# A batch-normalised matmul on one core: the order of its 782 tasks read from a table, and one small negation on GpSimd

## The chip, the core and the metric

The kernel runs on one core of a Trainium2 chip. The metric is device time in microseconds (us); the median of 3 runs of the kernel before is 206.29 us (206.23 to 206.86). Engines are written as in the profile: PE (TensorE matmul), PEld (its weight loads), DVE (VectorE), ACT (ScalarE), POOL (GpSimd), SP (SyncE, which here only issues DMAs).

## The reference

```python
def setup_inputs():
    batch, m, k, n = 16, 512, 1024, 768
    return {"x": randn(batch, m, k), "weight": randn(k, n), "gamma": ones(n), "beta": zeros(n), "eps": 1e-5}

def reference(x, weight, gamma, beta, eps):
    y = np.matmul(x, weight)
    mean = np.mean(y, axis=(0, 1), keepdims=True)
    var = np.var(y, axis=(0, 1), keepdims=True)
    return gamma * (y - mean) / np.sqrt(var + eps) + beta
```

All in float32. There are 8192 rows of y and 768 columns, and a column's mean and variance need all 8192 rows. So no element of a column can be written before the last matmul of that column is done.

## The kernel before

**Tiling.** The rows are 16 chunks (c = 0 to 15) of 512. The columns are six blocks of 128 (nt = 0 to 5, "column 0" to "column 5" below). Columns 0 and 1 are computed first, with rows on the partitions (`mm_rows`, L501 to L517), while x is still being loaded; columns 2 to 5 of chunks 0 to 3 are computed in this stage too. From about 97 us on the loads are over. Then come the last matmuls of columns 0 and 1 (`ga_unit`, L805, chunks 14 and 15), the sums and the scale and shift of these two columns (L865 to L915), and after that the rest of column 2, then 3, 4 and 5 (`col_unit`, L627, matmuls at L575, four weight tiles of 256 rows of k each, in two halves of four matmuls).

**One unit.** A unit (one chunk of one column) fills one of the 8 PSUM banks. Its statistics are taken (DVE bn_stats, L711; in column 2 from chunk 4 on two ACT passes with sums, L720 and L724), it is copied to SBUF as bf16 (ACT, L715), and then its bank is free. After a column's last unit, `finish_tasks` makes scale and shift (L976, L990, L993 to L998; for column 2 on ACT, L1004 to L1007, with the negated gamma of L964).

**Out again.** A finished column is normalised in SBUF (L1024 on ACT for column 2, L1026 on DVE for 3 and 4, L1348 for 5) and must be transposed back to rows: by a transposing DMA from the SP queue (L1220) and a copy to float32 on ACT (L1232); or on PE (`turn_block`, L1044, into a PSUM bank) and a copy on ACT (L1210, L1252, L1361). Some blocks are transposed raw beforehand (L1106) and normalised afterwards by DVE (L1174) and GpSimd (L1178). Columns 0 and 1 leave by DVE (L937), an add on GpSimd or DVE (L942) and a store (L946). All stores are issued by SP, in order, 512 KB each for the most part; the loads of x and of the weights by GpSimd. Two blocks of column 4 (chunks 14 and 15) are held back on purpose until the end (`held_block`, L1240).

**Riders.** The eight PE transposes of a column-4 block need not be a task of their own: a column-5 half may carry up to four of them, one after each of its matmuls (`mm`, L571 to L584). In the kernel before four blocks ride, four and four in consecutive halves.

**Who sets the order.** The code makes 786 tasks, each with a due time, possible engines with costs, dependencies, and the slots (PSUM banks, SBUF tiles, ring space) that it takes and uses. `arrange` (L122) is a greedy planner: it models the engines, the DMA queue (`Wires`) and a port that DVE tasks marked `lock` and GpSimd share (L162 to L165), and picks, at the earliest time at which some engine can begin something, the ready task with the smallest due time. The emitted instructions of each engine are then chained in this order by `seq` (L293), so each engine, and SP's queue of DMAs, runs its list in order; an instruction whose input is late holds up all that stand behind it on its engine.

**Names the change touches.** `negate_gamma` (L963, the task `ng`), whose result is read at L1004; `terms` (L1317), three small GpSimd instructions of column 5, first used at L1324; the copies of `part_chunk` (L547) that lay out chunks 12 to 15 plainly for columns 4 and 5 and may run on DVE or ACT.

Of the kernel before, what the change touches and what calls it, by code (L numbers as in the profile page):

```python
# [97 lines left out]
class Wires:  # L98
# [8 lines left out]
    def ready(self, queue):  # L107
        lanes = self.lanes[queue]
        return 0.0 if len(lanes) < self.LANES else lanes[-self.LANES]
# [9 lines left out]
        return t, land  # L119


def arrange(tasks, turns, log=None):  # L122

    free = {e: 1.25 for e in ("PE", "DVE", "ACT", "POOL", "SP")}
    wires = Wires()
    port = {"DVE": 0.0, "POOL": 0.0}
    left = sorted(tasks, key=lambda t: t.prio)
    order = []  # L130
    SEM, LOOK = 0.06, 0.2

    def ready(t):
        if t.after is not None and t.after.end is None:
            return None
        r = 0.0
        for d in t.deps:
            if d.end is None:
                return None
            r = max(r, d.end + SEM + t.slack)  # L140
        kept = [(s.pool, s.pool.mark()) for s in t.takes] if len(t.takes) > 1 else []
        fits = True
        for s in t.takes:
            p = s.pool.place(s)
            if p is None:
                fits = False
                break
            r = max(r, p[0] + SEM)
            if kept:
                s.pool.take(s, p[1])  # L150
        for pool, mark in reversed(kept):
            pool.reset(mark)
        if not fits:
            return None
        if t.dma:
            r = max(r, wires.ready(list(t.engines)[0]))
        return r

    def start_of(t, r, e):

        b = max(r, free[e])
        if e == "DVE" and t.lock:  # L162
            b = max(b, port["POOL"])
        elif e == "POOL" and not t.dma:
            b = max(b, port["DVE"])  # L165
        return b

    while left:
        seen = [(t, ready(t)) for t in left]
        first = {}  # L170
        for t, r in seen:
            if r is not None:
                for e in t.engines:
                    b = start_of(t, r, e)
                    if e not in first or b < first[e]:
                        first[e] = b
        if not first:
            raise RuntimeError(f"nothing can begin: {[(t.prio, t.emit) for t in left[:8]]}")
        e = min(first, key=lambda k: first[k])
        best = None  # L180
        for t, r in seen:
            if r is not None and e in t.engines and start_of(t, r, e) <= first[e] + max(LOOK, t.look):
                if best is None or t.prio < best[1]:
                    best = start_of(t, r, e), t.prio, t
        start, _, t = best
        for s in t.takes:
            s.pool.take(s, s.pool.place(s)[1])
        occ, lat = t.engines[e]
        t.hosted = []
        if t.hosts:  # L190
            room = t.hosts
            for u, r in seen:
                if u in turns and r is not None and r <= start + 0.3 and room >= 1:
                    n = min(room, turns[u][0])
                    if turns[u][0] == turns[u][1]:
                        places = [s.pool.place(s) for s in u.takes]
                        if any(p is None or p[0] > start for p in places):
                            continue
                        for s in u.takes:
                            s.pool.take(s, s.pool.place(s)[1])  # L200
                        u.takes_done, u.takes = u.takes, []
                    t.hosted.append((u, n))
                    turns[u][0] -= n
                    room -= n
                    occ += 0.0555 * n
                    lat += 0.0555 * n
        if t in turns:
            occ = lat = 0.0555 * turns[t][0]
            lat += 0.2
            t.count = turns[t][0]  # L210
        free[e] = start + occ
        if e == "DVE" and t.lock or e == "POOL" and not t.dma:
            port[e] = start + occ
        t.end = start + lat
        if t.dma:
            free[e], t.end = wires.send(e, start, occ, t.dma, t.count)
        t.start, t.engine = start, e
        order.append(t)
        left.remove(t)
        for u, n in t.hosted:  # L220
            if turns[u][0] == 0:
                u.end = t.end + 0.2
                left.remove(u)
    return order


# [1 line left out]
def kernel(  # L228
# [9 lines left out]
    nc = tc.nc  # L238
# [3 lines left out]
    ALU = mybir.AluOpType  # L242
# [5 lines left out]
    P = 128  # L248
# [44 lines left out]
    def seq(bi):  # L293

        ins = bi.ins
        prev = last.get(ins.engine)
        if prev is not None:
            tc.add_manual_dep(
                ins, prev,
                mybir.DependencyInfo(mybir.DependencyClass.NoSync, mybir.DependencyReason.DATA),  # L300
                reason="order",
            )
        last[ins.engine] = ins.name
        return bi

    gamma_sb = singles.tile([P, NT], f32)
# [28 lines left out]
    ngamma = singles.tile([P, NT], f32)  # L335
# [17 lines left out]
    tasks, turns = [], {}  # L353
    banks, xts, ys, sqs, rings = Pool(8), Pool(XT), Pool(YB), Pool(SQ), Space(RING)

    def task(prio, engines, emit, deps=(), lock=False, **kw):
        t = Task(prio, engines, emit, deps, **kw)
        t.lock = lock
        tasks.append(t)
        return t  # L360

    def dve(occ):
        return {"DVE": (occ, occ + 0.09)}
# [4 lines left out]
    def pool(occ):  # L368
        return {"POOL": (occ, occ + 0.05)}
# [70 lines left out]
    order = [("x", 0), ("w", 0, 2), ("x", 1), ("w", 2, 4)]  # L440
# [5 lines left out]
    t = 1.0  # L446
    affine = None
# [237 lines left out]
    def y_of(nt, c):  # L685
        return y_col.setdefault((nt, c // GY), Slot(ys))
# [174 lines left out]
    S = clock[0]  # L861
# [61 lines left out]
    sr = task(U + 0.1, dve(0.35), shift_rows, [sc], True)  # L923
# [32 lines left out]
    k = 0  # L956
# [4 lines left out]


    def negate_gamma(eng):  # L963
        seq(nc.vector.tensor_scalar(ngamma, gamma_sb, -1.0, None, op0=ALU.mult))  # L964

    ng = task(S, dve(0.1), negate_gamma, [affine, sr], True)

    def finish_tasks(nt):
        deps = [col_end[nt, c][0] for c in range(C)]
# [61 lines left out]
    def turn_block(prio, nt, m0, count, deps, uses):  # L1031

        bank = Slot(banks)
        todo = []

        def step():
            if not todo:
                o_ps = psum.tile([P, count, P], bf16, tag="b")
                bank.tile = o_ps
                for s in range(count):  # L1040
                    c, i = divmod(m0 // P + s, RT)
                    todo.append((o_ps[:, s], y(nt, c)[:, i * P:(i + 1) * P]))
            dst, src = todo.pop(0)
            seq(nc.tensor.transpose(dst, src, ident))  # L1044

        def emit(eng):
            for _ in range(emit.task.count):
                step()

        emit.step = step  # L1050
        t = task(prio, pe(0.0555 * count), emit, deps, takes=[bank], uses=uses)
        emit.task = t
        turns[t] = [count, count]
        return t, bank
# [213 lines left out]
    for nt in range(GA, NT - 1):  # L1268
# [10 lines left out]
        f = finish_tasks(nt)  # L1279
        start = clock[0] + 3.0  # L1280
# [58 lines left out]
    for c, r0, rows in ends:  # L1339
        due = E + 2.0 + 0.6 * c  # L1340
        n = max(rows // CH, 1)
# [13 lines left out]
        b, bank = turn_block(due + 0.6 * (n - 1), nt, m0, count, norms, [y_of(nt, c + i) for i in range(n)])  # L1355
# [7 lines left out]
        def store(eng, slot=slot, m0=m0, count=count):  # L1363
# [6 lines left out]
             uses=[slot])  # L1370

    order = arrange(tasks, turns)
    if "PLAN" in globals():
        PLAN.append(order)
# [37 lines left out]
```

## Time and profile before

The profiled execution has a span of 204.1 us from its first to its last instruction; the median of the three timed runs is 206.29 us, so 2.2 us lie around the span.

| engine | busy us | share of the span | instructions |
|---|---|---|---|
| PE | 189.3 | 93% | 1210 |
| DVE | 159.3 | 78% | 250 |
| ACT | 146.2 | 72% | 260 |
| POOL | 124.1 | 61% | 150 |
| DMA | 303 GB/s to and from HBM over the span | 36.7 MB read, 25.2 MB written | |

A row of the table of groups gives a line, an engine, an operation, how often, its busy time and the mean duration of one. A row of the timeline gives start, length, engine, line and operation; overlapping instructions of one line are merged. "Busy" for PE is modelled from the starts, so a stall of a few tens of nanoseconds doesn't show in it; the distance between starts does.

### The profile page before, as it was taken

How to read it: one execution, taken by the hardware profiler on the slowest of the kernel's cores; microseconds unless marked ns; L12 is line 12 of the kernel's file. 1: busy time of each engine (PE TensorE's matmuls, PEld its weight loads, DVE VectorE, ACT ScalarE, POOL GpSimd, SP SyncE). 2: the span in 40 equal slices, each digit the busy share in tenths (PEclk: the TensorE clock that was granted, in tenths of full speed). 3: DMA queues.
4: the chain of work that ended last, by engine and by line, in shares of the span. 5: the costliest groups of instructions: out<-in, count | busy, mean ns of one | idle time of the engine just before them, and what ended most of it. 6: DMA issues, size and time to landing. Idle time of an engine off the chain costs nothing.

```text
span 204.1 us, 3510 instructions
## 1 busy us (share of the span) xinstructions
PE 189.3 (93%) x1210; PEld 114.5 (56%) x1210; DVE 159.3 (78%) x250; ACT 146.2 (72%) x260; POOL 124.1 (61%) x150
## 2 busy tenths in 40 slices
PE   7969999999999999999999999999999999997900
PEld 3457554657488888777865444444444445544600
DVE  4031879999999999969989998987999878657900
ACT  2001461368989999899978766999998959956950
POOL 7776954877499989997403999389613312940000
PEclk9999999999999999999999999999999999999965
DMA  4999999999999999999686899899999999999998
GB/s 71 172 199 196 176 196 196 196 197 197 190 193 197 197 196 196 196 197 195 103 181 200 297 339 336 248 301 328 295 322 227 336 303 274 347 343 310 310 347 253
DMA packets 98562, 48.74 MB, mean 239 GB/s; under 512 B 24304, under 2 KB 98032, under 8 KB 98544
## 3 DMA queue, kind: packets, MB, share of 16 engines
q0 software_dynamic: 34624, 18.36, 65.5%
q1 hardware_dynamic: 63920, 30.16, 52.6%
q8 instruction: 9, 0.15, 0.3%
q14 instruction: 9, 0.07, 0.1%
HBM read 36.71 MB, written 25.17 MB: 303 GB/s over the span
## 4 chain that ended last, share of the span: by engine, by line
PE 86%; ACT 3%; DMA 3%; POOL 2%; issue 1%; ACTq 0%; DVE 0%; POOLq 0%
PE y_ps L575 54%; PE y_ps L510 24%; PE y_ps L814 4%; ACT o_sb L1361 3%; DMA ring<-in_x_dram 3%; PE o_ps L1044 1%; POOL ring L403 1%; POOL w_sb L387 1%; PE y_ps L753 1%; PE a_ps L903 1%; PE o_ps L1074 0%; ACTq L1407 0%; PE idle_ps L591 0%; PE tot_ps L871 0%; ACT ring L1252 0%
## 5 line engine op out<-in xcount | busy, mean ns | idle before, releaser
L575 PEld LDWEIGHTS <-w_sb 128*128 128x128 bf16 x520 | 50.3, 97 | 57.6
L575 PE MATMUL y_ps<-xT_sb,w_sb 128*128 128x512 bf16 (+1 forms) x272 | 59.3, 371 | 0.0
L575 PE MATMUL y_ps<-x_pl,w_sb 128*128 128x512 bf16 x248 | 57.4, 379 | 0.0
L403 POOL DMA_DIRECT2D ring<-in_x_dram x76 | 47.2, 626 | 14.4 <-DMA ring<-in_x_dram 5.5
L510 PE MATMUL y_ps<-w_sb,xT_sb 128*128 128x256 bf16 x448 | 50.6, 273 | 1.7 <-DMA ring<-in_x_dram 1.6
L510 PEld LDWEIGHTS <-xT_sb 128*128 128x128 bf16 x448 | 43.5, 98 | 9.4 <-DVE xT_sb L435 2.9
L435 DVE STREAM_TRANSPOSE xT_sb<-ring 128x1024 f32<-128x1024 f32 (+1 forms) x29 | 31.2, 1111 | 14.1 <-DMA ring<-in_x_dram 13.9
L711 DVE BATCH_NORM_STATS2 stats<-y_ps 128x6 f32<-128x512 f32 x46 | 30.9, 687 | 7.7 <-PE y_ps L575 7.2
L715 ACT CAST y_sb<-y_ps 128x512 bf16<-128x512 f32 x51 | 29.0, 593 | 10.4 <-DVE stats L711 6.3
L547 ACT COPY x_pl<-xT_sb 128x1024 bf16<-128x1024 bf16 x32 | 32.8, 1063 | 1.7 <-DVE xT_sb L435 1.7
L942 POOL TENSOR_TENSOR ring<-ring,sum 128x1024 f32<-128x1024 f32 (+1 forms) x11 | 23.8, 2188 | 14.9 <-ACT y_ps L724 10.9
L659 ACT ACTIVATE sq_sb<-y_ps 128x512 f32<-128x512 f32 x28 | 16.3, 610 | 16.2 <-PE y_ps L510 15.9
L666 POOL TENSOR_TENSOR sum<-sum,sq_sb 128x512 f32<-128x512 f32 x20 | 25.6, 1278 | 3.0 <-ACT sq_sb L659 1.7
L662 DVE TENSOR_TENSOR sum<-y_ps,sum 128x512 f32<-128x512 f32 x28 | 18.9, 675 | 6.3 <-ACT sq_sb L659 5.3
L672 ACT CAST y_sb<-y_ps 128x512 bf16<-128x512 f32 x28 | 16.3, 594 | 8.2 <-DVE sum L662 8.0
L1178 POOL TENSOR_TENSOR ring<-ring,sum 128x1024 f32<-128x1024 f32 x6 | 14.8, 2477 | 9.8 <-issue 8.5
L937 DVE TENSOR_TENSOR ring<-y_sb,a_ps 128x1024 f32<-128x1024 bf16 (+1 forms) x16 | 16.7, 1079 | 0.1
L1044 PE MATMUL o_ps<-ident,y_sb 128*128 128x128 bf16 x104 | 13.1, 221 | 1.6 <-DVE y_sb L1348 1.5
L1232 ACT CAST ring<-ring 128x1024 f32<-128x1024 bf16 x13 | 13.8, 1063 | 0.6 <-DMA ring<-y_sb 0.6
L1145 POOL COPY sum<-sum 32x256 f32<-32x256 f32 (+1 forms) x17 | 5.8, 340 | 13.4 <-DVE sum L1142 6.5
L428 DVE STREAM_TRANSPOSE xT_sb<-ring 128x2048 bf16<-128x2048 bf16 x6 | 13.5, 2290 | 0.1
L591 PE MATMUL idle_ps<-idle_sb 128*128 128x512 f32 x18 | 9.6, 688 | 1.5 <-DVE idle_sb L316 1.5
(104 smaller groups left out, 153.7 us busy)
## 6 DMA issues: line engine op xcount, KB each, us to landing
out_dram<-ring SPq DMA_DIRECT2D x37, 512.0 KB, 3.4
ring<-in_x_dram POOLq DMA_DIRECT2D x52, 256.0 KB, 8.8
out_dram<-o_sb SPq DMA_DIRECT2D x6, 512.0 KB, 4.7
ring<-in_x_dram POOLq DMA_DIRECT2D x16, 128.0 KB, 5.9
w_sb<-in_weight_dram POOLq DMA_DIRECT2D x8, 192.0 KB, 6.2
out_dram<-ring SPq DMA_DIRECT2D x6, 256.0 KB, 3.0
ring<-in_x_dram POOLq DMA_DIRECT2D x4, 192.0 KB, 7.8
out_dram<-o_sb SPq DMA_DIRECT2D x3, 256.0 KB, 2.5
```

The costliest lines, as they stand in the source:

```text
L403: bi = seq(nc.gpsimd.dma_start(x_bf[32 * i:32 * i + 32], src[:, :, KQ * i:KQ * (i + 1)]))
L435: seq(nc.vector.transpose(dst, src[:, :, jw0:jw1]))
L510: seq(nc.tensor.matmul(y_ps[:, s], x_of(c, jw, e, t * P, (t + 1) * P), w_sb[:, jw, e, 0:NA], start=(s == 0 and jw == 0 and e == 0), stop=( ...
L547: seq(nc.scalar.copy(dst, pairs) if eng == "ACT" else ENG[eng].tensor_copy(dst, pairs))
L575: seq(nc.tensor.matmul(y_ps, w_sb[:, jw, e, nt * P:(nt + 1) * P], moving(c, jw, e, q0 * QR, q1 * QR, parted), start=(jw == 0 and e == 0 an ...
L659: seq(nc.scalar.activation(sq_sb[:, 0:n], slot.tile[:, 0:n], AF.Square))
L662: seq(nc.vector.tensor_add(sum1, slot.tile[:, 0:n], sum1))
L666: seq(ENG[eng].tensor_add(acc, acc, state["sq"][:, 0:n]))
L711: seq(nc.vector.bn_stats(dst, slot.tile))
L715: seq(nc.scalar.copy(y(nt, c), slot.tile))
L937: seq(nc.vector.tensor_mul(slot.o, y_row[c].y[:, s0:s1], aff[0][:, None, :].to_broadcast([P, n, NA])))
L942: seq(ENG[eng].tensor_add(slot.o, slot.o, row[:, None, :].to_broadcast([P, n, NA])))
```

## The change

The greedy choice in `arrange` goes. In its place a table `ORDER` names every task by its number (in order of creation) after a letter for its engine (P PE, V DVE, A ACT, G POOL, S SP); what follows a plus sign are riders, "658.3" for three transposes of task 658. The costs, slots and dependencies stay: slots are still assigned by the same rule as the list is walked. The table came from a search in which transfers were made longer at random. And the negation of gamma is a GpSimd instruction.

```diff
+ORDER = (
+    "G0 P59 G3 G8 A9 G4 G7 V1 V2 P60 G10 P61 P62 P63 P64 P65 V5 V6 P66 G12 P67 P68 P69 P70 P71 G14 P76 A72 "
...
+    "A274 G54 A276 P403 P404 A281 V49 P405 A250 P406 P409 G278 V50 A261 P285 A262 V283 G57 V277 P290 A286 "
+    "V282 A279 V288 A284 V287 P410 A291 P411 V52 A289 G293 P412 A263 P415 G320 G321 G322 G381 P295 P298 V292 "
+    "V53 V319 V299 V296 A401 A413 A414 A264 A297 A402 A294 A300 A407 P304 P301 P323 V55 V58 V56 P310 P307 "
...
+    "V339 V336 V342 G340 G337 P420 P423 P389 P443 P435 P424 P444 P436 A390 A421 A422 A417 A445 A418 A437 A425 A446 "
+    "V345 V343 V351 V348 S341 S391 S344 S338 G346 G349 S347 P427 P439 P431 P440 P428 P432 P447 P448 A441 A426 "
+    "A429 A442 A433 A449 A434 V352 V354 S353 S350 G355 V360 V357 G358 S356 V361 V369 V363 A430 A438 A450 S362 "
...
+    "G542 V587 V606 V610 V602 V586 V585 V588 V589 V614 V591 G543 A550 A544 A603 A590 A611 A615 P620 P621 P632 "
+    "P633 P628 P629 P636 P637 S561 S557 S555 S551 V545 G546 A558 S547 V626 V618 V622 V634 V568 V564 V630 V638 "
+    "V641 S565 S559 A627 A631 A607 A642 A562 A635 A639 A619 A623 P673 P681 P682 P674 S569 V643 V661 V657 V644 "
+    "V665 V683 A566 A645 S563 P685+658.3 P689+662.1 P686+658.2,662.1 P677+662.1,658.1 P701+658.2,662.1 P678 "
+    "P690+662.4 S573 G646 A684 A570 A647 A659 S567 S571 V687 V651 V669 V648 V675 V679 V691 V654 S660 A574 "
+    "A663 A676 A688 A692 A680 S575 G652 G649 G655 P697 P698 P705 P706+670.3 P702+670.2,666.1 P709+670.1,666.2 "
+    "P693+666.1,670.2 P694+666.4 P713 P710 V707 V729 V695 V703 V699 V711 A671 A667 A708 A696 S664 S650 S656 "
+    "S653 S668 S672 P714 P717 P720 V723 V715 V718 V721 P730 P733 V724 V726 A712 A700 A704 A716 A731 A725 V728 "
...
+)
...
-    left = sorted(tasks, key=lambda t: t.prio)
+    left = tasks
     order = []
-    SEM, LOOK = 0.06, 0.2
+    SEM = 0.06
...
-    while left:
-        seen = [(t, ready(t)) for t in left]
...
-        start, _, t = best
+    NAMES = {"P": "PE", "V": "DVE", "A": "ACT", "G": "POOL", "S": "SP"}
+    for word in ORDER.split():
+        word, _, riders = word.partition("+")
+        t, e = left[int(word[1:])], NAMES[word[0]]
+        r = ready(t)
+        if r is None:
+            raise RuntimeError(f"out of order: {word}")
+        start = start_of(t, r, e)
...
-        if t.hosts:
...
+        for rider in riders.split(",") if riders else ():
+            i, n = rider.split(".")
+            u, n = left[int(i)], int(n)
...
     def negate_gamma(eng):
-        seq(nc.vector.tensor_scalar(ngamma, gamma_sb, -1.0, None, op0=ALU.mult))
-
-    ng = task(S, dve(0.1), negate_gamma, [affine, sr], True)
+        seq(nc.gpsimd.tensor_scalar(ngamma, gamma_sb, -1.0, None, op0=ALU.mult))
+
+    ng = task(S, pool(0.3), negate_gamma, [affine])
```

Set beside the order of the kernel before, engine by engine, the table reads as follows. Up to about 97 us every engine has the same list. From there on:

- PE: the same 196 tasks. The last two units of columns 0 and 1 and the sums change places (P304 P301 P323). The units of column 2 from chunk 9 on, of column 3, 4 and 5 are taken out of the order of their chunks, with halves of several units interleaved: P443 P435 P424 P444 P436 is chunk 14 (first half), 12, 9 (second half), 14, 12. In column 5 chunk 9 (P693, P694) is now among the last, and the riders are spread in ones, twos and threes; tasks 658, 662, 666 and 670 are the turns of column 4's chunks 6, 8, 10 and 12.
- DVE: statistics are later and normalisations earlier in many places. Of the sixteen copies of L547, DVE takes five that ACT had (V577 V579 V580 V586 V587) and ACT two that DVE had (A583 A584).
- ACT: the second passes of column 2 are put off (A434 A430 A438 A450 come last, together); the copies of the turned blocks of chunks 12 and 10 (A671 A667) come after four copies of column 5.
- POOL: G381, the negation, comes behind the sums; `terms` (727) moves from 99 us to behind the last add of column 2; two pairs of adds change places.
- SP: neighbouring stores and transposes change places; of the last six stores of column 4, S656 (the last GpSimd add of three) now stands ahead of S653, S668 and S672.

More of the change, by code (lines that the diff above doesn't have):

```diff
@@ L166, in start_of @@
         return b
-    while left:
-        seen = [(t, ready(t)) for t in left]
[L170 to L184, printed above, removed]
-        start, _, t = best
+    NAMES = {"P": "PE", "V": "DVE", "A": "ACT", "G": "POOL", "S": "SP"}
[6 more added lines that the diff above has]
+        start = start_of(t, r, e)
         for s in t.takes:
@@ L189, in arrange @@
         t.hosted = []
-        if t.hosts:
[L191 to L206, printed above, removed]
+        for rider in riders.split(",") if riders else ():
+            i, n = rider.split(".")
+            u, n = left[int(i)], int(n)
+            if turns[u][0] == turns[u][1]:
+                for s in u.takes:
+                    s.pool.take(s, s.pool.place(s)[1])
+                u.takes_done, u.takes = u.takes, []
+            t.hosted.append((u, n))
+            turns[u][0] -= n
+            occ += 0.0555 * n
+            lat += 0.0555 * n
         if t in turns:
@@ L218, in arrange @@
         order.append(t)
-        left.remove(t)
         for u, n in t.hosted:
@@ L222, in arrange @@
                 u.end = t.end + 0.2
-                left.remove(u)
     return order
```

24 rows, old and new, of the table ORDER are left out of this document.

## The prediction, on record before the changed kernel ran

> **What bounds the kernel now.** I read the chain of waits first, then the windows (busy time of PE, PEld, DVE, ACT, POOL; clock, DMA share, GB/s), then DMA's rate at the end, then the timelines of single engines. The chain (start, length, what), cut to its main pieces:
>
> ```profile
> 110.40 58.94 PE y_ps L575 x269
> ...
> 177.82 6.99 PE y_ps L575 x32
> 184.80 1.81 PE y_ps L753 x16
> 186.62 0.24 PE o_ps L1044 x4
> ...
> 189.60 4.74 ACT o_sb L1361 x6
> ```
>
> PE does matmuls one behind the other: 58.94 / 269 = 0.219 us each, with no other engine in the chain from 110 to 186.6 us. The windows say the same, and that DVE and ACT have little room:
>
> ```profile
> 120.00:130.00 10.00, 10.00 (x46) 4.26 (x45) 8.96 (x13) 7.63 (x22) 7.64 (x4) 1.00 0.84 297
> 140.00:150.00 10.00, 10.00 (x48) 4.46 (x46) 9.69 (x18) 10.00 (x15) 6.29 (x3) 1.00 1.12 309
> 150.00:160.00 10.00, 10.00 (x48) 4.48 (x46) 9.26 (x19) 8.72 (x13) 2.35 (x7) 1.00 1.19 274
> 180.00:190.00 10.00, 8.44 (x63) 4.87 (x60) 6.62 (x19) 5.63 (x13) 2.05 (x1) 1.00 1.07 322
> ```
>
> PE is 10.00 of 10 in each window up to 180, at granted clock 1.00: the matmuls can't be done sooner by reordering, only later. The rest is the tail, 204.1 - 186.6 = 17.5 us. DMA's rate from 165 to 204 us in 40 slices of 0.975 us:
>
> ```profile
> GB/s 347 346 337 287 304 347 304 85 348 345 348 348 346 347 347 345 344 333 347 347 346 346 349 185 282 299 244 338 346 348 347 345 349 345 347 347 348 345 228 0
> ```
>
> 347 GB/s is the ceiling. It is reached from 172.8 to 187.4, when column 4's last stores drain, and from 192.3 to the end. Between lie four slices of 185, 282, 299 and 244 and one of 338: (5 x 347 - 1348) / 347 x 0.975 = 1.1 us of idle DMA. Column 5 is 8192 x 128 x 4 bytes = 4.19 MB, 12.1 us at the ceiling; it can't begin before the chain behind the last matmul:
>
> ```profile
> 187.12 0.25 DVE L1308 BATCH_NORM_AGGREGATE mv<-fin 128x2 f32<-128x21 f32 x1
> ...
> 187.93 0.22 DVE L1324 SCALAR_TENSOR_TENSOR fss<-coef,rstd,base 128x2 f32<-128x2 f32 x1
> ...
> 189.31 10.56 SPq L1364 DMA_DIRECT2D out_dram<-o_sb  x11
> ```
>
> So the span is: PE's end, 2.7 us of small instructions to the first store, 12.1 us of bytes, and the holes. The order can win only from the 1.1 us of holes and from short gaps of PE before 110 us; it can lose wherever PE waits, where the small chain waits, or where column 4's stores outlast 187.4 by more than the holes.
>
> **The change part by part.** The order of before is read off the trace, that of after off the table.
>
> *Negation.* DVE loses one instruction of 0.16 us (group L964) at 107.5 us, where the next follows at once. GpSimd gets one on 128x6 float32. The nearest rows are its copies of 128x1, 0.18 us (L1318), and of 128x256 from 128x512 operands, 0.74 us (L795); I take 0.2, being nearest in size. It stands behind the sums, where GpSimd idles 10.85 us (before L942 at 110.46). Cost 0; without that cover 0.7 us of GpSimd, and its reader, L1004, comes only at 126 us. *terms*, three instructions (0.18, 0.10, 0.18 us), goes to a GpSimd idle stretch of 6 us after the add that ends at 146.3; its reader is L1324 at 187.9. Cost 0.
>
> *Sums, 96 to 107 us.* DVE does an add of 0.65 us ahead of the second transpose of chunk 14, which then ends near 97.56 + 0.62 = 98.2; its first matmuls move up to 98.5. Margin 0.3. The sums' matmuls start 0.9 later, but the chain to scale and shift hangs on the last bn_stats of chunk 15, whose matmuls end where they did. The block of chunk 15 is normalised second half first, so its first transpose starts up to 0.1 late. Cost 0.1; bounds -0.3 (the 0.31 us gap of PE behind the sums goes) and +0.4 (a bank comes late).
>
> *Column 2, 110 to 127 us.* The same 24 halves, 0.86 to 0.91 us each, so PE stands at the same place at 121.9. On ACT four second passes stand behind the last first pass (that begins at 122.06 before): 4 x 0.65 us, against one before, so L979 starts near 125.1 and not 123.25, and column 2's transposes begin some 1.5 us later. In return chunk 10's rows are multiplied and added on DVE (L937, L942) ahead of chunk 9's and stored earlier, into the windows' hole of 120 to 130 (DMA 0.84). Banks, counted by hand from table and durations: never more than 8 of 8, the tightest free one with 0.5 us to spare. Cost 0, and if that cover is gone 1.5 us of DMA idle, which later holes of before (0.65 us at 172) only partly take.
>
> *Columns 3 and 4, 123 to 166 us.* Three copies net go from ACT (1.05 us) to DVE (0.68): DVE +2.0 us. And DVE meets GpSimd's adds:
>
> ```profile
> 141.10 5.19 POOL L1178 TENSOR_TENSOR ring<-ring,sum 128x1024 f32<-128x1024 f32 x2
> 143.11 0.96 DVE L547 COPY x_pl<-xT_sb 128x1024 bf16<-128x1024 bf16 x1
> 145.76 0.54 DVE L993 SCALAR_TENSOR_TENSOR tmp<-mv,gamma_sb 128x1 f32<-128x1 f32 x1
> ```
>
> The copy takes 0.96 and not 0.68 where the first add ends at 143.5; the 0.16 us of L993 take 0.54, until just after the second ends at 146.29. Such a DVE instruction waits out the add, up to 2.4 us, and DVE's queue with it. In the new order the copies 577, 579 and 580 stand beside adds. Adding durations along DVE's list gives scale and shift of column 3 at 147.7 if DVE gets in between two adds, 149.4 if it loses each time (146.7 before). SP's first transposes of column 3 are issued at 152.25, so either is hidden; by banks PE doesn't wait in either case. I take the middle, cost 0. [...]
>
> *Column 5 and column 4's way out, 164 to 187 us.* The tightest place. Task 685, with the first rider, is fifth and not seventh in column 5: 163.8 + 4 x 0.864 = 167.2, its first transpose at 167.45. That needs the norm of chunk 6, second behind the shift, which ends at 166.15 (L997): 166.19 + 0.55 + 0.45 = 167.2. Margin 0.25. Before it was:
>
> ```profile
> 168.05 0.53 DVE L1026 TENSOR_SCALAR y_sb<-y_sb,scale,shift 128x1024 bf16<-128x1024 bf16 x1
> ...
> 169.18 0.22 PE L1044 MATMUL o_ps<-ident,y_sb 128*128 128x128 bf16 x1
> ```
>
> a margin of 0.6. The rider of chunk 10 ends at 182.05 (before 175.6) and that of chunk 12 near 181 (177.8), so ACT copies them at 181 to 183. The three GpSimd adds end near 180.6 (182.05 before). Ten stores of 512 KB are left from 172 us, 1.51 us each at 347 GB/s: 15.1 us, just what before has between 172.8 and 187.4. After, the first is issued near 170.5 and not 171.78; then DMA idles twice, 0.4 and 0.8 us, for the adds of S650 and S656, and ends near 187.5. The held blocks are issued at 187.53 anyway. Cost 0; up to 1.1 us more would fall into the holes.
>
> *Tail.* Chunk 9 is last but four: its bn_stats waits for PE until 182.05, and behind it stand three more, the sum-up, and two: 4 x 0.61 + 0.81 + 0.61 + 0.43 to 186.4, while the last bn_stats waits for PE until 186.66. Margin 0.27; ACT has 0.4. One ACT copy (L763) moves behind the held ones, ending by 188.8, before L1361 begins at 188.91. Cost 0; plus 0.5 if DVE is late.
>
> *Sum.* 0.1 us on the profiled 204.1, so 204.2; with the 2.2 us around the span (206.29 - 204.1) 206.4. A measurement of this kernel tells about 0.3%, 0.6 us, from no change.
>
> **The rivals.** *PE waits at the early rider (slower).* If DVE loses to each GpSimd add, its list after 149.4 stays 1.7 to 1.9 us late through 154 to 166 us, since it has work throughout; then column 4's shift ends near 168.0, the norm of chunk 6 at 169.0, and PE stands 1.5 us at task 685 with all of column 5 behind it: 207.9. It decides from 0.25 us of lateness on. For it: the rows above, DVE at 9.69 and 9.26 in 140 to 160. Against: DVE waits for PE 1.03 us just before column 4's last bn_stats (163.98). Chance 0.28.
>
> *The tail chain is late (slower).* DVE's list behind chunk 9 overruns its 0.27 us by some 0.5, or a bank of the sums by 0.4: 206.9. Chance 0.10.
>
> *The holes are filled (faster).* Were the first small stores of column 5 to find DMA busy with column 4's last and nothing then late, up to 1.1 us of holes go, and the 0.3 at the sums: 205.4 with 0.9 of both. For it: the holes are there. Against: bytes that fill them were done before 187.4 in the kernel before, so filling alone wins nothing; the first store must come sooner. Chance 0.15.
>
> *The table doesn't act as meant.* Slots might fall otherwise than counted, in banks above all, as units close in another order than they open; a late bank stops PE at once. The bank is one more way into the 207.9 and counted there.
>
> **How the numbers follow.** No change, 0.47; own range 206.0 to 206.9. The rider 0.28 at 207.9, the tail 0.10 at 206.9, the holes 0.15 at 205.4. The range goes from 205.5 to 208.0, the holes nearly whole and the rider whole. Slower by over 0.3%: the rider, half of the tail and a little of the forecast's upper end, 0.37; faster: the holes, 0.15; the rest 0.48.
>
> **What would show it.** PE starting L753 at 184.6 as now, and 10.00 in all windows from 110 to 180: right. A distance over 0.5 us between two starts of L575 near 167, released by L1026: the rider. The last bn_stats (L760) behind 186.7 with PE on time: the tail. A slice under 300 GB/s between 176 and 187 followed by the held stores landing late: my count of stores is wrong. If PE begins column 5 before 163.5, the premise that order can't speed PE is wrong.

## The result, and the profile after

The changed kernel ("after") takes 208.11 us (median of 6 runs, 207.60 to 208.58); the kernel before, on the same chip, 206.12 us (205.84 to 206.86). The ratio is 1.0095, 95% interval 1.0074 to 1.0115: slower by about 2.0 us, and outside the predicted range by 0.1 us. The profiled execution has a span of 206.1 us (before 204.1).

Lines of `after` lie 24 further down from `arrange` on: L575 is now L599, L711 is L735, L715 is L739, L1026 is L1050, L1044 is L1068.

Where the 2.0 us lie is read first from the windows (window; its length and PE's busy time, then PEld, DVE, ACT, POOL, each with a count; PE's granted clock, DMA share, GB/s):

```profile
140.00:150.00 10.00, 10.00 (x48) 4.49 (x46) 9.89 (x18) 7.80 (x13) 5.84 (x5) 1.00 1.00 300
150.00:160.00 10.00, 10.00 (x48) 4.48 (x46) 9.68 (x19) 8.87 (x13) 2.89 (x7) 1.00 1.09 234
160.00:170.00 10.00, 8.60 (x43) 3.68 (x41) 8.35 (x19) 5.34 (x10) 2.35 (x1) 1.00 1.10 295
```

PE is unbroken up to 160 us and loses 1.40 us in one window. DVE has no room left from 140 to 160, and DMA moves 234 GB/s where it moved 274. PE's timeline in that window (start, length, what, idle time before and its releaser) shows two gaps:

```profile
165.34 1.89 PE L599 MATMUL y_ps<-xT_sb,w_sb 128*128 128x512 bf16 x8 [0.54 <-ACT y_sb L739]
...
169.17 0.23 PE L1068 MATMUL o_ps<-ident,y_sb 128*128 128x128 bf16 x1 [0.86 <-DVE y_sb L1050]
```

By the distance of starts they are 0.70 us (task 681 of column 5, which waits for the PSUM bank that ACT's copy 627 frees) and 1.03 us (task 685, whose first rider waits for the norm of chunk 6, L1050). Together that is 1.73 us, and PE's last unit ends at 188.36, not 186.62: 1.74 us later. The tail is 206.1 - 188.36 = 17.7 us against 17.5. The chain of waits tells what stands behind both gaps (start, length, what):

```profile
154.06 0.96 ACT ring L1256
155.03 5.75 DMA out_dram<-ring
160.88 1.22 DVE ring L1198
162.09 2.40 DVE stats L735 x4
...
168.11 1.01 DVE y_sb L1050 x2
170.43 0.86 PE y_ps L599 x4
```

Before, nothing but PE stood in the chain from 110 to 186.6 us. Now it runs through a store of column 2 (task 489) that needs 5.75 us to land, through DVE's task 545 (`norm_raw`, L1198), which waits for that store's place in the ring (the SBUF buffer in which outgoing blocks lie until their store has landed), and along DVE's list to the norm that PE waits for. Why the store lands late stands in SP's timeline, first of the kernel before, then of after:

```profile
149.75 1.77 SPq L1106 DMA_TRANSPOSE r_sb<-y_sb  x1
151.61 0.54 SPq L1202 DMA_DIRECT2D out_dram<-ring  x1
152.25 3.03 SPq L1220 DMA_TRANSPOSE ring<-y_sb  x2
155.37 0.54 SPq L1202 DMA_DIRECT2D out_dram<-ring  x1
```

```profile
148.22 6.03 SPq L1244 DMA_TRANSPOSE ring<-y_sb  x3
154.34 1.16 SPq L1226 DMA_DIRECT2D out_dram<-ring  x2
155.55 3.67 SPq L1130 DMA_TRANSPOSE r_sb<-y_sb  x1
159.27 2.73 SPq L1244 DMA_TRANSPOSE ring<-y_sb  x2
```

The store 485, issued at 151.61 before, stands in the table behind the transposing DMA 549. That DMA waits for a norm (548: the normalisation of a block, L1050), which DVE ends only at 152.99, and SP holds the store until 154.34; from 153 to 154 us DMA moves 2 GB/s. Two stores and the raw transpose (L1130, at 149.75 before) then come at once, and the transpose 557 is issued at 160.75, before at 156.00. ACT pays for this too: its convert (L1256, the copy of a transposed block to float32; task 558) waits 3.93 us for that transpose, with the bank-freeing copy 627 behind it:

```profile
163.76 1.04 ACT L1256 CAST ring<-ring 128x1024 f32<-128x1024 bf16 x1 [3.93 <-DMA ring<-y_sb]
164.72 0.58 ACT L739 CAST y_sb<-y_ps 128x512 bf16<-128x512 f32 x1
```

The view of the waits of DVE between 123 and 167 us (what waits, for what, total, times, longest) shows how little it could give, first before, then after:

```profile
DVE stats L711 <- PE y_ps L575: 3.2, 4, 1.0
DVE ring L1174 <- DMA out_dram<-ring: 1.3, 2, 0.7
```

```profile
DVE ring L1198 <- DMA out_dram<-ring: 1.1, 1, 1.1
DVE stats L735 <- PE y_ps L599: 0.3, 1, 0.3
```

DVE's wait for PE is its slack: 3.2 us before, 0.3 us after. With 0.3 us, the wait of 1.06 us for the store goes straight on to the column's scale and shift; without it, in f1, the shift comes 1.15 us earlier.

Where the slack went shows in the stretch from the start of the sums' last turns to the end of column 4's shift (a row of the windows, and the group of the plain copies in it), first before, then after:

```profile
107.11:166.15 59.04, 59.04 (x285) 26.81 (x284) 53.56 (x86) 51.22 (x99) 35.91 (x28) 1.00 1.02 293
L547 DVE COPY x_pl<-xT_sb 128x1024 bf16<-128x1024 bf16 x8 | 5.5, 715 | 0.0
```

```profile
107.05:168.07 61.02, 60.48 (x291) 27.32 (x289) 59.11 (x88) 47.70 (x96) 37.45 (x31) 1.00 1.00 286
L571 DVE COPY x_pl<-xT_sb 128x1024 bf16<-128x1024 bf16 x11 | 11.2, 1036 | 0.1
```

DVE is busy 59.11 us and not 53.56, so 5.55 us longer, and its idle time falls from 5.48 us to 1.91, of which 1.06 is the ring wait. Three copies more, at 0.68 us each, are 2.0 of the 5.55. Most of the rest is DVE instructions that lie beside a GpSimd add and end only after it: the copies 577, 579 and 580 took 1.35, 2.58 and 1.84 us, where 578, which began ahead of the next add, took 0.68; and a copy of 128x32 (L1165) took 2.35 us (0.64 before) and ended at 133.69, the add beside it at 133.65.

### The profile page after: what moved, and what is told of

Its sections match the earlier page's. It is cut to its first block, busy times and chain, and to the rows that moved or that the text cites. A ratio compares the mean times of both kernels' runs of the same rounds, so it can differ in the third digit from the quotient of the medians.

```text
span 206.1 us, 3500 instructions
## 1 busy us (share of the span) xinstructions
PE 190.5 (92%) x1210; PEld 115.8 (56%) x1210; DVE 166.3 (81%) x252; ACT 142.1 (69%) x257; POOL 125.6 (61%) x151
## 4 chain that ended last, share of the span: by engine, by line
PE 59%; DMA 15%; DVE 10%; ACT 5%; POOL 3%; issue 2%; SPq 1%; ACTq 1%; DVEq 0%; POOLq 0%
PE y_ps L599 30%; PE y_ps L534 21%; DMA w_sb<-in_weight_dram 6%; PE y_ps L838 4%; DVE stats L735 3%; DMA ring<-y_sb 3%; DMA ring<-in_x_dram 3%; DMA out_dram<-ring 3%; PE o_ps L1068 2%; DVE y_sb L1372 2%; DVE ring L1198 2%; ACT y_sb L1047 1%; POOL ring L1202 1%; POOL ring L427 1%; SPq L1244 1%
## 5 line engine op out<-in xcount | busy, mean ns | idle before, releaser
L599 PEld LDWEIGHTS <-w_sb 128*128 128x128 bf16 x520 | 49.9, 97 | 57.0 <-issue 0.8
L599 PE MATMUL y_ps<-xT_sb,w_sb 128*128 128x512 bf16 (+1 forms) x272 | 60.9, 371 | 0.5 <-ACT y_sb L739 0.5
L599 PE MATMUL y_ps<-x_pl,w_sb 128*128 128x512 bf16 x248 | 58.3, 379 | 0.0
L739 ACT CAST y_sb<-y_ps 128x512 bf16<-128x512 f32 x51 | 27.9, 587 | 8.0 <-DVE stats L735 5.9
L966 POOL TENSOR_TENSOR ring<-ring,sum 128x1024 f32<-128x1024 f32 (+1 forms) x11 | 24.3, 2235 | 12.3 <-DVE ring L961 12.3
L571 ACT COPY x_pl<-xT_sb 128x1024 bf16<-128x1024 bf16 x29 | 29.8, 1057 | 2.5 <-DVE xT_sb L459 1.7
L735 DVE BATCH_NORM_STATS2 stats<-y_ps 128x6 f32<-128x512 f32 x46 | 29.5, 681 | 1.6 <-PE y_ps L599 1.6
L696 ACT CAST y_sb<-y_ps 128x512 bf16<-128x512 f32 x28 | 16.1, 600 | 7.9 <-DVE sum L686 7.6
L1068 PE MATMUL o_ps<-ident,y_sb 128*128 128x128 bf16 x104 | 13.6, 243 | 3.2 <-DVE y_sb L1372 2.3
L1256 ACT CAST ring<-ring 128x1024 f32<-128x1024 bf16 x13 | 13.5, 1051 | 4.0 <-DMA ring<-y_sb 3.9
L1068 PEld LDWEIGHTS <-y_sb 128*128 128x128 bf16 x104 | 8.4, 110 | 6.2 <-DVE y_sb L1372 3.3
```

What stands on the lines that cost most here:

```text
L571: seq(nc.scalar.copy(dst, pairs) if eng == "ACT" else ENG[eng].tensor_copy(dst, pairs))
L599: seq(nc.tensor.matmul(y_ps, w_sb[:, jw, e, nt * P:(nt + 1) * P], moving(c, jw, e, q0 * QR, q1 * QR, parted), start=(jw == 0 and e == 0 an ...
L735: seq(nc.vector.bn_stats(dst, slot.tile))
L739: seq(nc.scalar.copy(y(nt, c), slot.tile))
L966: seq(ENG[eng].tensor_add(slot.o, slot.o, row[:, None, :].to_broadcast([P, n, NA])))
```

## The experiments

Task numbers: 485 and 489 are column 2's last two turned blocks' stores; 549, 553, 557, 561 the transposing DMAs of column 3's blocks and 550, 554, 558 the converts (L1256) of the first three of these; 603, 611, 615, 627, 631 copies of column 4 (L739) that free banks; 590 a plain copy (L571) on ACT; 657 and 661 the norms of column 4's chunks 6 and 8. Only the words of the table that change are shown.

**e1, the negation alone.** The order before as a table, and:

```diff
-        seq(nc.vector.tensor_scalar(ngamma, gamma_sb, -1.0, None, op0=ALU.mult))
+        seq(nc.gpsimd.tensor_scalar(ngamma, gamma_sb, -1.0, None, op0=ALU.mult))
```

> The order of the kernel before, written as a table, with the negation alone on GpSimd behind the sums. Theory: the negation costs nothing, 206.1 us, ratio 1.000 within 0.002, and PE has no wait from 110 us on. Rival: the negation on GpSimd delays the scale of column 2 or the adds behind it, and gives part of the 2 us: 206.5 or more.

Measured: 205.79 us, ratio 1.000 (0.9987 to 1.0012). The negation costs nothing; the loss is the order's.

**e2, riders later.**

```diff
-P685+658.3 P689+662.1 P686+658.2,662.1 P677+662.1,658.1 P701+658.2,662.1 P678
+P685 P689+662.1 P686+658.3,662.1 P677+662.1,658.2 P701+658.2,662.1 P678+658.1
```

> After, with the three riders of chunk 6 taken off task 685 and put on later halves (686, 677, 678); nothing else is moved. Theory: of after's 1.73 us the 1.03 us at task 685 go, the 0.70 us at task 681 stay: 207.1 us, PE's end at 187.3. Rival A (DVE is late as a whole, and a PSUM bank stops PE a little later): PE's end stays at 188.3 and the time at 208.1. Rival B (the last transposes then come late in the tail): 207.5 or more.

Measured: 207.77 us (206.80 to 208.78), ratio 1.0103 (1.0074 to 1.0132). The rider's wait is gone in the profiled execution and so is that at task 681, but one of 1.08 us has come at 159.7: from the waits of PE (window 110 to 192), and from ACT's timeline:

```profile
PE y_ps L599 <- ACT y_sb L739: 0.9, 1, 0.9
```

```profile
157.80 1.05 ACT L1256 CAST ring<-ring 128x1024 f32<-128x1024 bf16 x1 [1.85 <-DMA ring<-y_sb]
...
159.06 0.58 ACT L739 CAST y_sb<-y_ps 128x512 bf16<-128x512 f32 x1
```

In this execution the transposing DMA 549 landed late: convert 550 began at 157.80 (in after's at 155.88, with no wait), and the copy 603 behind it freed its bank at 159.64. The orders are the same up to there, so this is a difference between executions: the DMA, issued at 153.01 in both, landed 2.8 us later in after and 4.7 us later here, and the order passes that on to PE. Neither the theory nor its rivals had it. Rival B came in part as well: from the start of PE's last unit to the end of the span e2 takes 20.1 us, the kernel before 19.5; but f2 takes 20.1 with after's riders, so the late riders are not shown to be the reason.

**e3, copies first.**

```diff
-A615 A558 ... A627 A631 A607
+A615 A627 A631 A558 ... A607
```

> After, with the copies of chunks 12 and 13 of column 4 (627, 631) put ahead of column 3's convert (558) on ACT; nothing else is moved. Theory: the 0.70 us at task 681 go, but the norm of chunk 6 still ends at 169.1, so the rider's wait grows from 1.03 to about 1.7 us and the sum stays: 208.1 us within 0.2, PE's end at 188.3. Rival (the two waits add up independently): 207.4 us.

Measured: 208.72 us, ratio 1.0161 (1.0134 to 1.0187). As expected the bank's wait goes and the rider's grows, but to 2.4 us: copy 631 needs a bn_stats that ends at 165.94, so 558 and the root behind it (the square root for column 4's scale, ACT, L1014) came 0.6 us later, and the norm of chunk 6 ended at 169.74. The edit moved one copy too many, and the time is 0.4 us above what the theory allowed.

**e4, both.** The edits of e2 and e3 together.

> After, with both edits, riders later and copies first. Theory: both waits go, PE is on the schedule of the kernel before to the end (its end at 186.6 to 186.8): 206.4 us, ratio to before 1.001. Rival (a later bank takes their place, DVE being 1.7 to 1.9 us late): 207 us or more, with PE waiting for DVE's statistics in column 5.

Measured: 208.32 us, ratio 1.0125 (1.0105 to 1.0145): the rival. The next rider (662, task 689) waited 1.4 us instead, for a bank that an ACT copy of L739 frees. Taking waits away at PE's end of the chain does not help while DVE and ACT are late.

**f1, the store first.**

```diff
-S487 S553 S549 S485
+S487 S553 S485 S549
```

> After with one word moved: on SP the store 485 of column 2 is ahead of the transposing DMA 549 that waits for a norm, not behind it. Theory (the store held up behind 549 is the root): 485 is issued at 151.8 and not 154.3; DVE's wait for ring space at task 545 (1.06 us) goes, column 4's shift ends at 167.1 (not 168.1), the norm of chunk 6 at 168.1 (not 169.1). PE's waits add up to 0.6 to 0.7 us and not 1.73: PE's end at 187.3, 207.0 us. Rival (DVE is late by its own work alone, three copies more and the waits for GpSimd): DVE's list is where it was at 166, 208.1 us.

Measured: 207.79 us (206.19 to 208.62), ratio 1.0090 (1.0066 to 1.0114): by the median nearer to the rival. In the profiled execution, which at 206.19 us is the fastest of the six, the mechanism is as expected; DVE's timeline:

```profile
159.38 1.22 DVE L1198 TENSOR_TENSOR ring<-r_sb,a_ps 128x1024 f32<-128x1024 bf16 x1
...
166.36 0.21 DVE L1021 SCALAR_TENSOR_TENSOR shift<-tmp,rstd,beta_sb 128x1 f32<-128x1 f32 x1
```

No wait before task 545, the shift at 166.57 and not 168.08 (this execution was 0.36 us earlier as a whole from the loads on, so 1.15 us of it are the edit's), and one wait of PE, at the rider, 0.58 us. The median is hardly better; the next run's profile suggests why.

**f2, also the norms swapped.**

```diff
-V643 V661 V657 V644
+V643 V657 V661 V644
```

> The kernel of f1 with one more move: the norm of chunk 6, which the first rider needs, ahead of that of chunk 8 on DVE. Theory: the first rider's norm ends at 167.6, and its wait is 0.15 us or nothing; what is left is a wait for a bank at task 681 if ACT's convert is still late: 206.4 us, 207.0 with the bank. Rival (PE waits elsewhere in column 5): no better than f1.

Measured: 207.53 us (206.29 to 208.30), ratio 1.0077 (1.0051 to 1.0102). The profiled execution (207.64 us) has no wait at the rider, and one of 1.22 us at 159.80 behind convert 550, which waited 1.98 us for the landing, as in e2. The runs reach from about the expected time to 1.9 us above it, more than this one wait, and by the interval the rival, no better than f1, is not excluded. It may be a price of this SP list: in the seven profiled executions with the store behind 549, that DMA landed 2.8 us after its issue in six and 4.7 in one (e2); in the seven with the store ahead of it, 3.0 to 3.2 us in three (f1, h3, i2) and 4.6 to 5.5 in four (f2, f4, h4, i3).

**f3, copies back.**

```diff
-V580 ... V586 ... V587 ... A583 ... A584
+A580 ... A586 ... A587 ... V583 ... V584
```

> After with the late plain copies on the engines of the kernel before: 580, 586, 587 on ACT, 583 and 584 on DVE; stores and transposes in after's order. Theory (ring space): DVE reaches task 545 earlier, but waits there until 160.9 all the same; column 4's shift at 168.0, 208.1 us within 0.4. Rival (the copies and their wait for GpSimd are what makes DVE late): the shift ends at 167 or before, 207 us or less.

Measured: 208.42 us, ratio 1.0120 (1.0107 to 1.0133): the theory. DVE came 0.6 us earlier to task 545 and waited there 0.9 us longer:

```profile
161.14 1.22 DVE L1198 TENSOR_TENSOR ring<-r_sb,a_ps 128x1024 f32<-128x1024 bf16 x1 [1.96 <-DMA out_dram<-ring]
```

Column 4's shift ended at 168.34. The copies are not the root as long as the ring sets the time. The test is not a clean one: on ACT the copies held up the convert ahead of the store 489, which was issued at 156.14 and not at 155.03 (and landed at 161.04, after's at 160.78).

**f4, f2 and f3 together.**

> All three: store first, norms swapped, late copies back. Theory: DVE ends column 4's shift near 166.5, no wait for the rider is left, and the converts on ACT are on time: PE on the schedule of the kernel before, 206.2 us within 0.4. Rival (column 2's late transposes or the tail cost something by themselves): 206.8 or more with PE's end at 186.7.

Measured: 207.28 us (206.42 to 208.28), ratio 1.0066 (1.0040 to 1.0092). That is neither the theory nor the rival, which had PE's end at 186.7. In the profiled execution the wait at 159.7 (1.06 us) stands once more; nothing at the rider. DVE came to task 545 at 159.20 with no wait for the ring, and then waited 0.8 us for PE, which the bank had held up; so this run does not tell what the copies alone cost.

**h1, converts behind copies.** Ring places are written out as after has them.

```diff
-A554 A550 A544 A603 A590 A611 A615 A558 ... A627
+A554 A544 A603 A590 A611 A615 A550 A627 A558
```

> After with two moves on ACT alone: the convert 550 behind the bank-freeing copies 603, 611 and 615 of column 4, and the copy 627 ahead of the convert 558 (ring places kept as in after). Theory: no bank stops PE at 159 or 165 any more, but DVE is as late as in after, so the norm of chunk 6 still ends at 169.1 and the first rider at 167.4 waits for all of it, 1.7 us: 208.1 us within 0.3, and a narrower spread than the kernels of the runs before. Rival (the waits for banks are a loss of their own): 207.4 or less.

Measured: 208.05 us (207.91 to 208.34), ratio 1.0108 (1.0095 to 1.0121): time, spread and place as expected. No bank stops PE, and the whole wait stands at the rider, 1.68 us by starts:

```profile
PE o_ps L1071 <- DVE y_sb L1053: 1.5, 1, 1.5
```

**h2, the riders late too.** On top of h1, tasks 685, 689 and 686 have no rider of 658 and 662, and:

```diff
-P677+662.1,658.1 P701+658.2,662.1 P678 P690+662.4
+P677+658.2,662.2 P701+658.2,662.2 P678+658.2,662.2 P690+658.2,662.2
```

> The kernel of h1, and the riders of chunks 6 and 8 all moved to tasks 677, 701, 678 and 690, from about 169.8 us on; DVE, GpSimd and SP have after's lists. Theory: DVE is as late as in after (column 4's shift ends at 168.1) and it costs nothing, since PE asks for nothing of it before 169.8: no wait of PE over 0.2 us, PE on the schedule of the kernel before, 206.3 us within 0.4. Rival (later banks of column 5 stop PE, because ACT's copies 635, 639, 619 and 623 stand behind the late root): 206.9 or more.

Measured: 208.20 us, ratio 1.0113 (1.0097 to 1.0129): the rival. PE runs unbroken to 174.7 us and then pays in three places, for banks of turned blocks (L1237) and of a unit (L742):

```profile
PE y_ps L602 <- ACT ring L1237: 1.2, 2, 0.8
PE o_ps L1071 <- ACT y_sb L742: 0.5, 1, 0.5
```

**h3, f2 with h1's moves; h4, its riders later as well.** Ring places from here on are those of f2. For h4:

```diff
-P685+658.3 P689+662.1 ... P677+662.1,658.1 P701+658.2,662.1 P678 P690+662.4
+P685 P689+658.1 ... P677+658.2,662.2 P701+658.2,662.2 P678+658.1,662.2 P690+662.1
```

> The kernel of f2 (store 485 ahead of 549, norms swapped) with h1's two moves on ACT. Theory: the execution-to-execution wait of 1.1 to 1.2 us at 159.7 (a bank behind convert 550) is gone, and the first rider's norm ends at 167.5, 0.1 after PE is there: 206.2 us within 0.4, with a spread of 0.6 like the kernel before. Rival (other waits of column 5): 207 or more.

> The kernel of h3 with the riders beginning one task later (689) and spread in ones and twos up to task 690. Theory: no wait of PE between 110 us and its end, 206.1 us within 0.4; after's order without its waits is then worth no more than the order before. Rival (the filled windows of DMA at 120 to 130 and the changed tail are worth something): 205.5 or less, faster than the kernel before.

Measured: 207.37 us, ratio 1.0072 (1.0057 to 1.0086), and 207.84 us, 1.0091 (1.0078 to 1.0104). Neither tested what it was meant to. Convert 550 now ran at 160, and in these kernels it reads from the ring place that task 545 is to write: in h3 the convert ends at 161.00 and 545 begins at 161.09, as late as in after. They say only that a wait of DVE there makes column 4's shift as late as in after (1.97 and 1.99 us), whatever makes the wait.

**i2, without that side effect.** f2, and

```diff
-A554 A550 A544 A603 A590 A611 A615 A558 ... A627
+A554 A544 A603 A611 A550 A590 A615 A627 A558
```

> The kernel of f2 (store 485 ahead of 549, norms swapped); on ACT only the copies 603 and 611 go ahead of convert 550 (590 and 615 stay behind it), and 627 ahead of 558. Convert 550 then ends by 159.2 whatever the landing, before DVE is at task 545 (159.8), whose ring place it has to leave first. Theory: neither the bank at 159.7 nor the ring at 545 nor the rider waits more than 0.15 us; column 4's shift ends near 167.0, PE's end at 186.7 to 187.0: 206.3 us within 0.4, spread under 1 us. Rival (a loss of after's order that is in none of the waits named): 207 or more.

Measured: 206.78 us (205.88 to 207.51), ratio 1.0041 (1.0025 to 1.0057): just above what the theory allowed, and below the rival. In the profiled execution PE has no wait left between 110 us and its last unit; the window, and the only wait of DVE (123 to 167 us) besides 0.2 us for the root:

```profile
160.00:170.00 10.00, 9.95 (x51) 4.56 (x50) 8.76 (x21) 6.96 (x12) 2.37 (x1) 1.00 1.16 317
```

```profile
DVE stats L738 <- PE y_ps L602: 0.3, 1, 0.3
```

**i3, the riders of h4 on top.**

> The kernel of the run before this one (f2, copies 603, 611 and 627 early) with the riders beginning one task later (689) and spread to 690, as in h4. Theory: no wait of PE from 110 us to its end, and the time of the kernel before: 206.0 us within 0.4. Rival: a bank or a late copy in column 5 still stops PE for 0.5 us or more, 206.6 or more.

Measured: 206.46 us (205.76 to 206.95), ratio 1.0023 (1.0008 to 1.0038). The median lies between theory and rival. The profiled execution, 206.71 us, has 0.85 us of waits for banks near 176 to 178, as the rival has it; the median is the best of all versions of this order, and not below the kernel before.

**i4, the other way round.** The order before with e1's negation, and in SP's list

```diff
-S485 S549 S553
+S549 S553 S485
```

> The other way round: the kernel before (its order as a table, the negation on GpSimd), with the store 485 put behind the transposing DMAs 549 and 553, as late as after has it (issued near 154.8 and not 151.6). Theory: task 545 waits some 1 us longer for ring space on DVE, but DVE there waits 1.0 us for PE before column 4's last statistics, and no bank-freeing copy stands behind a convert that waits: 206.0 us within 0.3, PE without a wait. Rival (a store held up behind a waiting transposing DMA costs time by itself): 206.6 or more.

Measured: 206.13 us (205.92 to 207.03), ratio 1.0012 (0.9997 to 1.0027): the time of the theory. DVE waits 1.3 us for the ring at task 545 and still has 2.4 us of slack. But e1, the same order with the store early, is the run to set beside it, and its profiled execution has a longer ring wait and as little slack; DVE's waits from 123 to 167 us, first of e1, then of i4:

```profile
DVE stats L735 <- PE y_ps L599: 2.3, 4, 1.0
DVE ring L1198 <- DMA out_dram<-ring: 1.7, 1, 1.7
```

```profile
DVE stats L735 <- PE y_ps L599: 2.4, 4, 1.0
DVE ring L1198 <- DMA out_dram<-ring: 1.3, 1, 1.3
```

So the ring wait of i4 can't be put down to the edit (the kernel before had 0.55 us there, e1 1.7, in one and the same order of stores). What the two runs show is that this order pays 1.3 and 1.7 us of ring wait from its slack: PE's last unit starts on time in both.

Side by side, in profiled executions. Both delays are measured from the start of the sums' last turns (L927, near 107.0) and against the kernel before: that of column 4's shift on DVE (end of L1021) and that of PE's last unit (L777).

| kernel | shift late, us | PE's last unit late, us | ratio of times |
|---|---|---|---|
| after | 1.99 | 1.80 | 1.0095 |
| f3 copies back | 2.13 | 1.93 | 1.0120 |
| h1 converts behind | 1.94 | 1.84 | 1.0108 |
| h2 and riders late | 2.08 | 2.14 | 1.0113 |
| f1 store first | 0.84 | 0.65 | 1.0090 |
| i2 store first, swapped, copies early | 0.85 | 0.19 | 1.0041 |
| i3 and riders later | 0.83 | 0.85 | 1.0023 |
| i4 before, store late | 0.01 | 0.01 | 1.0012 |
| e1 negation alone | 0.03 | 0.01 | 1.0000 |

The delays are those of one execution, the ratios those of the medians. In f1 the two differ most: its profiled execution is its fastest.

## Why the prediction was wrong, and where it was right

*The failed step is "Columns 3 and 4, 123 to 166 us".* It put the shift of column 3 between 147.7 and 149.4 and took the middle, 148.55; it ended at 148.78. It then said that this is hidden, since SP's first transposes of column 3 are issued at 152.25, and "by banks PE doesn't wait in either case", cost 0. Neither held: column 4's shift came 1.93 us later by the clock (1.99 from the sums), and PE lost 0.70 us at a bank and 1.03 at the rider.

First, it worked out DVE's list for column 3 alone and did not follow it on to column 4. The copies and the waits beside GpSimd's adds, which it saw rightly, cost DVE 5.55 us of busy time where 5.48 were idle before. Second, it let SP's list count for nothing though it had changed: 152.25 is a time of the old order, and in the table the transposing DMA 549 stands ahead of the store 485, and its norm 548, which followed column 3's shift directly before, has seven DVE tasks ahead of it there, four of them norms. From there come the 1.06 us of ring wait. f1's profiled execution takes back 1.15 of the shift's 1.99 us by moving one store. The other 0.84 us are put down to DVE's own added work by the account of its busy time (59.04 of 59.88 us in f1); no run took this work away with everything else on time. Third, it had banks free by durations, not by who stands behind whom: a copy that frees a bank stood behind a convert that waits for a DMA, 3.93 us in after.

*The rider rival was right in place and in size, and partly by luck.* It named a shift near 168.0 and a norm at 169.0; they came at 168.08 and 169.11. But its condition, that DVE loses to each GpSimd add and column 3's shift ends at 149.4, did not come, and of column 4's 1.99 us of lateness 1.15 went with the store, which it does not name. It gave 1.5 us at the rider; the rider waited 1.03, since the bank had held PE up 0.70 before it, and h1, without the bank's wait, shows 1.68. So 207.9 stood against 208.11 measured. Its chance, 0.28, was too low: the one thing held against it, DVE's wait of 1.03 us for PE just before column 4's last statistics, was slack of the kernel before, and the added work and the ring wait had used it.

*Column 5's margin of 0.25 us* was worked out from 166.15, the shift of the kernel before. In the table's order the shift came 1.93 us later, so there was no margin.

*Negation: right* (e1). *Sums: right*; the last turns start at 107.05, before at 107.11, less than two executions of one order differ (e1 107.04). *Column 2: right for PE*, which is on its schedule to 163.77 (before 163.78). *Tail: right in size*; it is 0.2 us longer, not shortened by a filled hole. The split of the tail given at the outset does not close, though: 186.6 + 2.7 + 12.1 + 1.1 is 202.5, not 204.1, and what it leaves out are the held blocks' two stores of 256 KB, issued at 187.53, 1.5 us at 347 GB/s. The forecast starts from the measured span, so nothing hangs on it. The 347 GB/s called a ceiling are the rate of the last stores, at which column 5 did leave (346 to 347 GB/s from 192.3 to 202 us before); elsewhere DMA moved more, 384 GB/s from 118 to 120 us before and 385 from 112 to 120 us after. *"PE can't be sped by order": right*; no version came below the kernel before (ratios 1.0000 to 1.0161).

*What is settled, and what is not.* The waits named are most of the loss: with them removed the ratio falls from 1.0095 to 1.0041 (i2) and 1.0023 (i3), so about 1.1 to 1.5 of 2.0 us. That the bank's wait and the rider's are one loss, DVE's lateness, is shown by h1: without the first, the second is as long as both. What the store does shows in the profiled executions: with it behind 549, DVE waits 0.6 to 2.0 us at task 545 in all seven; with it ahead, in f1, f2, f4, i2 and i3, not at all. f1's median doesn't show it; in times it shows from h1 (1.0108) to i2 (1.0041), which differ in the store, in the two norms, and in smaller moves on ACT and in the ring. That the order before can pay for a ring wait is shown by e1 and i4.

Open are the last 0.8 us of i2 and 0.5 us of i3 (0.2 to 0.8 by its interval). In i3's profiled execution the bank waits are all of it: PE's last unit is 0.85 us late and what follows takes 19.5 us, as before. In i2's the last unit is 0.19 us late and the rest 0.5 us longer, and no run tells why. Why the transposing DMA 549 landed 2.8 to 3.2 us after its issue in nine profiled executions and 4.6 to 5.5 us after it in five, and late in four of seven with the store ahead of it against one of seven with the store behind, is open too.

## What to carry to other kernels

Before you call a delay hidden, add up how long the late engine waits for the bound one (here DVE for PE: 3.2 and 2.3 us in two executions of the order before, 0.3 after): that slack, and not a margin at one place, is what a wait can be paid from. In an order that each engine runs strictly, look at every instruction that waits for a DMA or a late engine and ask what stands behind it; a copy that frees a bank, or a store that frees a buffer, does not belong behind one where that slack is gone. A wait taken away at the bound engine's end of such a chain came back here at the next place that needed the late engines (1.4 us in e4, 1.2 and 0.5 us in h2), so look for the first link.

## What had not been expected of the hardware

PE's clock fell after a gap. In e3's profiled execution PE stood still for 2.4 us at 167.4, and its granted clock was 0.50 from about 170.8 to 174.2, 3.4 us (windows of 1 us, the clock behind POOL's count; a mean of 0.91 is counted as 0.18 us at 0.50 and the rest at 1.00, the two values that whole windows show):

```profile
170.00:171.00 1.00, 0.95 (x8) 0.55 (x7) 0.20 (x1) 1.00 (x4) 0.00 (x0) 0.91 1.24 297
171.00:172.00 1.00, 1.00 (x5) 0.42 (x4) 0.90 (x2) 1.00 (x3) 0.00 (x0) 0.50 1.17 337
...
174.00:175.00 1.00, 1.00 (x7) 0.41 (x5) 0.55 (x1) 0.69 (x2) 0.26 (x1) 0.89 1.20 326
```

That execution took 210.28 us, the kernel's others 208.49 to 209.39. h1's gap of 1.7 us near 168 was followed by 1.00 up to 176 us. In the tail, where PE waits 1.5 to 1.6 us for the last scale and shift (1.53 before, 1.62 after), the clock fell to 0.50 for about 3.4 us in the profiled executions of after, e1 and i2, and not before 195 us in that of the kernel before; e1 has the same order there as the kernel before, so it is by execution. i2 moved 200 GB/s from 190 to 191 us and 228 from 193 to 194, where the kernel before moved 254 and 348, and its tail is 0.5 us longer than before's (19.96 against 19.46 from the last unit's start); e1's is not (19.52), so the fall of the clock alone does not make it longer.
